# Which rows of a chunked scan TensorE transposes, and which go by VectorE transposes and DRAM

## The chip, the cores and the metric

The kernel runs on one core of one Trainium2 chip. The metric is device time of one launch in microseconds (us), the median over several executions. The work of a core is spread over TensorE (PE; its weight loads are listed apart as PEld), VectorE (DVE), ScalarE (ACT), GpSimd (POOL) and SyncE (SP). Each engine takes its own instructions strictly in the order in which they stand in the program and waits on semaphores for the others. Nearly all transfers of this kernel are issued from SP's queue.

## The reference

One step of a hybrid decoder layer in float32: RMSNorm, one wide projection, two branches (a Mamba-2 scan and a short gated convolution), a sigmoid-gated sum, an output projection and a last RMSNorm. There are 336 tokens: 16 learned ones and 256 of a prompt in one sequence, and 8 sequences of 8. The change touches the scan:

```python
xbc_c, conv_new = causal_dwconv(xbc, conv_prev, ssd_conv_w)
xbc = jax.nn.silu(xbc_c + ssd_conv_b)
xs, bm, cm = jnp.split(xbc, [D_INNER, D_INNER + SSD_GROUPS * SSD_STATE], axis=-1)
...
cb = jnp.einsum('bcign,bcjgn->bcijg', cc, bc)
wts = cb[..., None] * decay * dtc[:, :, None]
y_diag = jnp.einsum('bcijgr,bcjgrp->bcigrp', wts, xc)
chunk_states = jnp.einsum('bcjgr,bcjgrp,bcjgn->bcgrpn', to_end, xc, bc)
```

The projection leaves channels on the partitions and tokens along the row, and the convolution works that way. The products over tokens j need the same values with tokens on the partitions: xc (4 tiles of 128 channels in each of the 8 groups) and bc (one tile of 128 states). So five tiles of 128 channels x 336 tokens have to be turned in each group, in chunks of 128, 128 and 80 tokens.

## The kernel before, in words

All weights are split into two reduced-precision parts. A weight tile of 128 columns is read in two halves, which this text calls blocks and marks a and b. For one block, `wblk` loads 512 KB to `wraw` (line 92, SP), ACT rounds it to `whi` (line 94), DVE subtracts to `wlo` (line 96), and TensorE runs 16 matmuls with `whi` (lines 111 and 112) and then 8 with `wlo` (line 115). `wraw`, `whi` and `wlo` have three buffers each, so a block can be prepared while TensorE works on the blocks before it.

The scan runs in 8 stages, one for each group g. `weave` strings a stage's projections together: the gate z of group g (blocks z0a to z3b, the evacuation by ACT is lines 502 and 503), the output product of group g-1 (8 blocks), in two stages some branch gates, and then the projections of group g+1 with their convolution (`conv_tile`, blocks BTa to x3b). Between these units it places the steps of the generator `ssd(g)`, which yields after each step. `behind` ties the ACT, DVE and TensorE instructions of a step behind the latest block that was traced; within these ties a scheduler lays down each engine's final order when the program is built.

`conv_tile` projects, has ACT copy the result to a padded tile and apply the first tap with its bias (lines 462, 463, 469; tile `cacc`, two buffers), DVE add three taps (line 471), ACT take a tanh (line 474) and DVE write the result (lines 475, 476) to `BT`, `CT` or a quarter of `xs`.

In `ssd`, the steps `rows(0)`, `rows(1)`, `rows(2)` turn one chunk each: four transposes of `xs` by TensorE (line 534), one of `BT` (line 536), one product of B and C (line 537); DVE multiplies the turned x by dt to `xdt` (line 539), ACT and DVE split the turned B (lines 546, 547), DVE masks the product (line 551). `decay` and `weights` make the decay matrices, `state` and the 64 products of line 650 use them all. Near the stage's end stand the grouped norm (`ms_r`, lines 700 to 705; `yh`, `yl`, lines 726 to 728) and the states of the 8 short sequences, whose tiles `h` are loaded at line 607 (`h0T`, 4 transfers of 512 KB), added to at line 716 and stored at line 719 (`ssms`, 4 transfers of 512 KB). These transfers stand in SP's queue among the weight loads.

Of the kernel before, what the change touches and what calls it, by code (L numbers as in the profile page):

```python
# [7 lines left out]
F32 = mybir.dt.float32  # L8
F32R = mybir.dt.float32r
AF = mybir.ActivationFunctionType  # L10
# [3 lines left out]
P = 128  # L14
T = 336
# [7 lines left out]
HP = 64  # L23
# [4 lines left out]
DUM = 14  # L28
WARM = 10
NSTEP = 23  # L30

C_ID, C_U, C_M1, C_UQ, C_M1Q, C_ONE = 0, 128, 272, 400, 480, 560
C_SEG = 688
# [5 lines left out]
def fb(ap):  # L39
    return ap.bitcast(F32)  # L40


def bc(ap, shape):
    return ap.to_broadcast(shape)
# [3 lines left out]
def tile_hybrid_step(ctx, tc, xT, w0, w1, w2, wdt, wso, wsc, wo, cmask, vec, hvec, convst, sconvst, xe_, fwe, h0T,  # L48
                     yA, yB, yE, convo, ssmp, ssms, sconvo):
    nc = tc.nc  # L50
    mult, add, sub = ALU.mult, ALU.add, ALU.subtract
# [3 lines left out]
    ps = ctx.enter_context(tc.tile_pool(name="ps", bufs=2, space=PSUM))  # L55
    dr = ctx.enter_context(tc.tile_pool(name="dr", bufs=1, space=bass.MemoryType.DRAM))

    ac_d = [dr.tile([NH, n], F32, name=f"ac_d{c}") for c, n in enumerate((P - META, PX, 80))]
    mb_d = dr.tile([KT, P, TV], F32, name="mb_d")
    sg_d = dr.tile([KT, P, TV], F32, name="sg_d")  # L60
    xq_d = [dr.tile([80, 4, 512], F32, name=f"xq_d{i}") for i in range(2)]
    bq_d = [dr.tile([80, 4, P], F32, name=f"bq_d{i}") for i in range(2)]

# [11 lines left out]
    ident = CM[:, C_ID:C_ID + P]  # L75
# [12 lines left out]
    latest = {}  # L88

    def wblk(src, n=1024):  # L90
        raw = wp.tile([P, 1024], F32, name="wraw")
        nc.sync.dma_start(raw[:, :n], src)
        hi = wp.tile([P, 1024], F32R, name="whi")
        latest["act"] = nc.scalar.activation(hi[:, :n], raw[:, :n], AF.Copy).ins  # L94
        lo = wp.tile([P, 1024], F32R, name="wlo")
        latest["dve"] = nc.vector.tensor_tensor(lo[:, :n], raw[:, :n], fb(hi[:, :n]), sub).ins  # L96
        return hi, lo

    def behind(tail):
        for ins in reversed(nc.cur_bb.bb.instructions):  # L100
            if ins is tail:
                break
            for a in latest.values():
                if ins.engine == a.engine:
                    tc.add_manual_dep(ins, a.name, mybir.DependencyInfo(mybir.DependencyClass.NoSync,
                                                                         mybir.DependencyReason.DATA), reason="step")

    def mm(out, hi, lo, xh, xl, base, nk, k0, first, last):
        for k in range(nk):
# [14 lines left out]
    def proj(src, t0):  # L124
        return unit(src, lambda k: hhi[:, k, t0:T], lambda k: hlo[:, k, t0:T], T - t0)
# [35 lines left out]
    act = keep.tile([P, 3, NH], F32, name="act")  # L161
    dtt = keep.tile([P, 3, NH], F32, name="dtt")
# [7 lines left out]
    with tc.tile_pool(name="pa", bufs=2) as pa:  # L170
# [4 lines left out]
        raw = []  # L175
# [28 lines left out]
        for k in range(KT):  # L204
# [5 lines left out]
            if k % 2 == 0 or k == 1:  # L210
                o = slice(384 * k, 384 * k + 384) if k < 2 else slice(0, 768)
# [233 lines left out]
    def hv(ap, g):  # L445
        return ap[:, 8 * g:8 * g + 8].unsqueeze(2)

    with tc.tile_pool(name="pb", bufs=2) as pb:
# [5 lines left out]
        nc.gpsimd.memset(CZ, 0.0)  # L454
        czs = CZ.rearrange("p (s i w) -> p s i w", s=2, w=40)

        def conv_tile(src, j, t0, out, cs):
            pp = proj(src, t0)
            pad = pads[npad[0] % 2]
            npad[0] += 1  # L460
            smp = pad[:, 275:363].rearrange("p (b t) -> p b t", t=11)
            nc.scalar.activation(pad[:, 3 + t0:275], pp[:, :272 - t0], AF.Copy)  # L462
            nc.scalar.activation(smp[:, :, 3:11], pp[:, 272 - t0:].rearrange("p (b t) -> p b t", t=8), AF.Copy)
            nc.gpsimd.tensor_copy(smp[:, :, 0:3], cs[:, 1:9, :])  # L464
            nc.gpsimd.tensor_copy(cs[:, 0, :], pad[:, 272:275])  # L465
            nc.gpsimd.tensor_copy(cs[:, 1:9, :], smp[:, :, 8:11])
            i0 = META if t0 else 0
            acc = pb.tile([P, 360], F32, name="cacc")
            nc.scalar.activation(acc[:, i0:], pad[:, i0:360], AF.Identity, bias=col(V_CB, j), scale=col(V_CW, 4 * j))
            for k in range(1, 4):  # L470
                nc.vector.scalar_tensor_tensor(acc[:, i0:], pad[:, i0 + k:360 + k], col(V_CW, 4 * j + k),  # L471
                                               acc[:, i0:], mult, add)
            th = pb.tile([P, 360], F32, name="cth", bufs=1)
            nc.scalar.activation(th[:, i0:], acc[:, i0:], AF.Tanh)
            nc.vector.scalar_tensor_tensor(out[:, i0:272], th[:, i0:272], 1.0, acc[:, i0:272], add, mult)
            nc.vector.scalar_tensor_tensor(
                out[:, 272:].rearrange("p (b t) -> p b t", t=8),
                th[:, 272:360].rearrange("p (b t) -> p b t", t=11)[:, :, 3:11], 1.0,
                acc[:, 272:360].rearrange("p (b t) -> p b t", t=11)[:, :, 3:11], add, mult)

        def conv_units(g, st):
            cs = pb.tile([P, 6, 9, 3], F32, name="cs")
            nc.sync.dma_start(cs, convst[:, g])
            BT = st["BT"] = pb.tile([P, T], F32, name="BT")
            conv_tile(w1[64 + g], 32 + g, 0, BT, cs[:, 4])
            yield
            CT = st["CT"] = pb.tile([P, T], F32, name="CT")
            conv_tile(w1[72 + g], 40 + g, 12, CT, cs[:, 5])
            yield
            xs = st["xs"] = pb.tile([P, 4, T], F32, name="xs", tag=f"xs{g % 2}", bufs=1)  # L490
            for t in range(4):
                conv_tile(w1[32 + 4 * g + t], 4 * g + t, 0, xs[:, t, :], cs[:, t])
                yield
            nc.sync.dma_start(convo[:, g], cs)

# [12 lines left out]
        def big(tag, bufs, dt=F32):  # L508
            return pb.tile([P, 512], dt, name=tag, bufs=bufs)

        def split(ap, w=HP):
            return ap.rearrange("p (h e) -> p h e", e=w)

        def ssd(g, st):
# [3 lines left out]
            xw = free[:, :1024].rearrange("p (i n) -> p i n", n=512)  # L518
            h0, h0t = [], []
            ys = pb.tile([P, 4, T], F32, name="ys", bufs=1)  # L520
            W, xdt, xe, bt, cbm, hst = ([None] * 3 for _ in range(6))
            W[0], W[1] = (pb.tile([P, 8, PX], F32, name="W")[:, :, :n] for n in (P - META, PX))
            W[2] = pb.tile([P, 8, 80], F32, name="W2", bufs=1)
            E = pb.tile([P, 8, PX], F32, name="E", bufs=1)
# [2 lines left out]
                nc.sync.dma_start(w[:r], ac_d[c][8 * g:8 * g + 8, :].partition_broadcast(r))  # L527
            NT, TGT = (P - META, PX, 80), (META, P, 2 * P)

            def rows(c):  # L530
                (t0, n), m = CH[c], NT[c]
                pp = ps.tile([P, 512], F32, name="ms")
                for t in range(4):
                    nc.tensor.transpose(pp[:n, t * P:t * P + P], xs[:, t, t0:t0 + n], ident)  # L534
                pq = ps.tile([P, 512], F32, name="ms")
                nc.tensor.transpose(pq[:n, 0:P], BT[:, t0:t0 + n], ident)
                nc.tensor.matmul(pq[:n, P:P + m], BT[:, t0:t0 + n], CT[:, TGT[c]:TGT[c] + m], start=True, stop=True)
                xdt[c] = big("xdt", 3)
                nc.vector.tensor_tensor(split(xdt[c][:n]), split(pp[:n]), bc(hv(dtt[:n, c, :], g), [n, 8, HP]), mult)
                if c == 2:  # L540
                    bt[c] = pb.tile([P, P], F32, name="bt", bufs=1)
                    nc.scalar.activation(bt[c][:n], pq[:n, 0:P], AF.Copy)
                else:
                    bt[c] = (free[:, 1024:1280].rearrange("p (i n) -> p i n", n=P) if c else
                             pb.tile([P, 2, P], F32R, name="bh0", bufs=1))
                    nc.scalar.activation(bt[c][:, 0, :], pq[:, 0:P], AF.Copy)
                    nc.vector.tensor_tensor(bt[c][:, 1, :], pq[:, 0:P], fb(bt[c][:, 0, :]), sub)
                cbm[c] = pb.tile([P, PX], F32, name="cbm")
                u0 = META if c == 0 else 0
                for a, b, o in ((0, m, 0),) if c < 2 else ((META, 80, 0), (0, META, 64)):  # L550
                    nc.vector.tensor_tensor(cbm[c][:n, o:o + b - a], pq[:n, P + a:P + b],
                                            U[:, u0 + a:u0 + b] if c < 2 else UQ[:, a:b], mult)

            def decay(c):
                n, m, w = CH[c][1], NT[c], W[c]
                for h in range(8):
                    a = act[:n, c, 8 * g + h:8 * g + h + 1]
                    if c:
                        nc.scalar.activation(w[:n, h, :], w[:n, h, :], AF.Relu, scale=-1.0, bias=a)  # L559
                    else:  # L560
                        nc.vector.tensor_scalar(w[:n, h, :], w[:n, h, :], a, 0.0, sub, ALU.min)
                nc.scalar.activation(w[:n], w[:n], AF.Exp, scale=-1.0 if c else 1.0)
# [33 lines left out]
                    nc.gpsimd.tensor_tensor(split(h0[b]), split(h0[b]), bc(hv(decS[:, b, :], g), [P, 8, HP]), mult)  # L596

            yield
            rows(0)
            yield  # L600
            decay(0)
            yield
            nc.scalar.activation(E, W[1], AF.Exp)
            rows(1)
            for u in range(4):
                h = pb.tile([P, 2, 512], F32, name="h0", bufs=4)
# [429 lines left out]
```

## Time and profile before

| what | before |
|---|---|
| median of 3 runs | 1823.18 us (1822.88 to 1823.36) |
| profiled execution, its own time | 1824.75 us |
| its span, first to last instruction | 1823.0 us |
| TensorE busy | 1814.9 us of the span |
| VectorE busy | 1147.7 us |
| ScalarE busy | 828.8 us |
| granted TensorE clock | 1.0 |
| SP's DMA queue, share of 16 engines | 55.9% |

A row of the timeline reads: start in us from the span's start, length, engine, line and operation, what is written and read, how many equal ones follow each other, and in brackets how long the engine had been idle and what ended that. A row of a group gives the busy time in all and the mean of one in ns, then the idle time before it. "SPq" rows are DMA issues: their length is the issue, not the transfer. Matmuls overlap, so what one costs TensorE is read from the distance of two starts and not from its length.

### The profile page before, as it was taken

What the parts mean: (1) busy time and instruction counts of PE and PEld (TensorE: products, weight loads), DVE (VectorE), ACT (ScalarE), POOL (GpSimd) and SP (SyncE); (2) the same over time, 40 slices, a digit from 0 to 9 for tenths busy, and PEclk for the clock granted to TensorE, in tenths of its full rate; (3) what the DMA queues carried; (4) which work ended last, traced back from release to release, by engine and by line L of the source; (5) the groups of instructions that cost most, each with busy time, mean ns of one, the idle gap of its engine ahead of it and who ended that gap; (6) DMA issues with size and microseconds to landing.
All of it is one profiled execution on the core that took longest, in us unless ns stands there. A gap on an engine that the chain in (4) does not pass through costs nothing.

```text
span 1823.0 us, 32410 instructions
## 1 busy us (share of the span) xinstructions
PE 1814.9 (100%) x13006; PEld 1798.0 (99%) x13006; DVE 1147.7 (63%) x1696; ACT 828.8 (45%) x1269; POOL 389.4 (21%) x398
## 2 busy tenths in 40 slices
PE   9999999999999999999999999999999999999998
PEld 9999999999999999999999999999999999999998
DVE  7745544444543335668587787877778777776544
ACT  6433333333333334645656354564546545343543
POOL 0000000000000001253162433524334252400012
PEclk9999999999999999999999999999999999999999
DMA  7444444444444446457566574665656657476553
GB/s 254 146 151 150 150 149 149 145 152 151 156 152 159 160 162 227 149 178 240 163 201 223 177 246 150 208 215 178 238 157 211 206 169 249 153 243 213 184 175 129
DMA packets 117286, 331.33 MB, mean 182 GB/s; under 512 B 20944, under 2 KB 37904, under 8 KB 117136
## 3 DMA queue, kind: packets, MB, share of 16 engines
q1 hardware_dynamic: 116272, 327.89, 55.9%
q8 instruction: 102, 1.67, 0.4%
q10 hardware_dynamic: 864, 1.38, 0.2%
q14 instruction: 48, 0.39, 0.1%
HBM read 296.34 MB, written 32.88 MB: 181 GB/s over the span
## 4 chain that ended last, share of the span: by engine, by line
PE 96%; DMA 2%; ACT 1%; DVE 1%; issue 0%; POOLq 0%; POOL 0%; SPq 0%; ACTq 0%; DVEq 0%
PE pj L111 30%; PE pj L112 30%; PE pj L115 29%; PE yb L650 2%; DMA wraw<-w 1%; PE ms L636 1%; PE pj L219 1%; PE yb L585 1%; PE pj L862 1%; ACT whi L94 0%; PE ms L534 0%; ACT W L559 0%; PE ms L219 0%; DMA ssms<-h 0%; PE yb L713 0%
## 5 line engine op out<-in xcount | busy, mean ns | idle before, releaser
L111 PE MATMUL pj<-hx,whi 128*128 128x320 f32 (+3 forms) x2880 | 864.4, 312 | 0.0
L112 PE MATMUL pj<-hx,whi 128*128 128x320 f32 (+3 forms) x2880 | 860.6, 311 | 0.0
L96 DVE TENSOR_TENSOR wlo<-wraw,whi 128x1024 fp32r<-128x1024 f32 x470 | 596.8, 1270 | 413.9 <-ACT whi L94 206.8
L94 ACT ACTIVATE whi<-wraw 128x1024 fp32r<-128x1024 f32 x470 | 496.7, 1057 | 768.0 <-PE pj L112 628.1
L111 PEld LDWEIGHTS pj<-hx,whi 128*128 128x128 f32 x2880 | 540.7, 188 | 4.6 <-ACT pad L462 1.7
L112 PEld LDWEIGHTS pj<-hx,whi 128*128 128x128 f32 x2880 | 541.5, 188 | 0.1
L115 PE MATMUL pj<-hx,wlo 128*128 128x320 f32 (+3 forms) x2880 | 485.4, 310 | 0.0
L115 PEld LDWEIGHTS pj<-hx,wlo 128*128 128x128 f32 x2880 | 440.6, 188 | 0.0
L111 PE MATMUL pj<-yh,whi 128*128 128x320 f32 x512 | 153.5, 311 | 1.2 <-ACT zs L503 0.9
L112 PE MATMUL pj<-yl,whi 128*128 128x320 f32 x512 | 152.3, 309 | 0.0
L596 POOL TENSOR_TENSOR h<-h,decS 128x512 f32<-128x512 f32 x64 | 76.4, 1227 | 147.5 <-PE ms L636 147.5
L111 PEld LDWEIGHTS pj<-yh,whi 128*128 128x128 f32 x512 | 96.2, 188 | 3.1 <-ACT zs L503 1.4
L112 PEld LDWEIGHTS pj<-yl,whi 128*128 128x128 f32 x512 | 96.3, 188 | 0.6
L115 PE MATMUL pj<-yh,wlo 128*128 128x320 f32 x512 | 95.8, 309 | 0.0
L242 POOL COPY SCS<-up 128x2 f32<-128x2 f32 x16 | 18.2, 1139 | 359.2 <-DVE up L236 329.0
L744 DVE TENSOR_TENSOR yan<-yan,pj 128x320 f32<-128x320 f32 x112 | 54.2, 485 | 62.9 <-PE pj L115 61.3
L471 DVE SCALAR_TENSOR_TENSOR cacc<-pad,V,cacc 128x360 f32<-128x360 f32 (+1 forms) x144 | 89.5, 621 | 2.0
L464 POOL COPY pad<-cs 128x24 f32<-128x24 f32 x48 | 56.2, 1172 | 126.6 <-DVE cacc L471 115.5
L115 PEld LDWEIGHTS pj<-yh,wlo 128*128 128x128 f32 x512 | 80.4, 188 | 0.0
L111 PE MATMUL pj<-vhi,whi 128*128 128x320 f32 x256 | 75.5, 308 | 0.0
L112 PE MATMUL pj<-vlo,whi 128*128 128x320 f32 x256 | 75.5, 308 | 0.0
L465 POOL COPY cs<-pad 128x3 f32<-128x3 f32 x48 | 45.0, 938 | 82.5 <-ACT pad L462 82.0
(286 smaller groups left out, 1721.7 us busy)
## 6 DMA issues: line engine op xcount, KB each, us to landing
wraw<-w SPq DMA_DIRECT2D x346, 512.0 KB, 3.9
wraw<-wso SPq DMA_DIRECT2D x64, 512.0 KB, 3.5
wraw<-wsc SPq DMA_DIRECT2D x32, 512.0 KB, 3.8
h<-h0T SPq DMA_DIRECT2D x32, 512.0 KB, 4.9
ssms<-h SPq DMA_DIRECT2D x32, 512.0 KB, 4.2
wraw<-wo SPq DMA_DIRECT2D x32, 512.0 KB, 3.9
xq_d<-xe SPq DMA_DIRECT2D x16, 320.0 KB, 3.4
W<-ac_d SPq DMA_DIRECT2D x8, 576.0 KB, 6.4
```

Source lines behind the costliest of these rows:

```text
L94: latest["act"] = nc.scalar.activation(hi[:, :n], raw[:, :n], AF.Copy).ins
L96: latest["dve"] = nc.vector.tensor_tensor(lo[:, :n], raw[:, :n], fb(hi[:, :n]), sub).ins
L111: nc.tensor.matmul(out, w, xh(k0 + k), start=first and k == 0, stop=False)
L112: nc.tensor.matmul(out, w, xl(k0 + k), start=False, stop=False)
L115: latest["pe"] = nc.tensor.matmul(out, w, xh(k0 + k), start=False, stop=last and k == nk - 1).ins
L219: nc.tensor.matmul(pu[i][:, :T - t0], w[:, o:o + P], x[:, k, t0:], start=k == 0 and j == 0, stop=k == 15 and j == 2)
L464: nc.gpsimd.tensor_copy(smp[:, :, 0:3], cs[:, 1:9, :])
L465: nc.gpsimd.tensor_copy(cs[:, 0, :], pad[:, 272:275])
L471: nc.vector.scalar_tensor_tensor(acc[:, i0:], pad[:, i0 + k:360 + k], col(V_CW, 4 * j + k), acc[:, i0:], mult, add)
L596: nc.gpsimd.tensor_tensor(split(h0[b]), split(h0[b]), bc(hv(decS[:, b, :], g), [P, 8, HP]), mult)
L650: nc.tensor.matmul(yb[q * HP:(q + 1) * HP, t, t0:t0 + n], x[:, h * HP:(h + 1) * HP], w[:, h, :], start=i == 0, stop=i == 3)
L744: nc.vector.tensor_tensor(ya[:, m, :TV], ya[:, m, :TV], pp[:, :TV], add)
```

## The change

B and the first two of the four x tiles are turned another way. After their convolution, DVE transposes the tile in 32x32 squares (two instructions, one of 320 columns and one of 32) into the tile `cacc`, and four DMAs write the squares to a scratch tensor in DRAM, `xr_d` (352 rows of 384 floats, in pieces of 32 floats), so that its rows are tokens. `pend` holds each tile's writes back until two more tiles have been projected, and `after` ties them behind the latest weight load of that moment. A new function `load` reads a chunk's rows back to `xdt` and to the B tile in three steps of the stage; `decay(0)` moves one step forward. `rows` keeps two TensorE transposes and the product of B and C, and multiplies x by dt in two halves. `behind` ties the same three engines as before.

```diff
     def wblk(src, n=1024):
         raw = wp.tile([P, 1024], F32, name="wraw")
-        nc.sync.dma_start(raw[:, :n], src)
+        latest["sp"] = nc.sync.dma_start(raw[:, :n], src).ins
...
-        def conv_tile(src, j, t0, out, cs):
+        pend = []
+
+        def conv_tile(src, j, t0, out, cs, rows=None):
             pp = proj(src, t0)
+            for p in pend:
+                p[0] -= 1
+            while pend and not pend[0][0]:
+                _, to, frm = pend.pop(0)
+                for a in range(0, P, 32):
+                    after(nc.sync.dma_start(to[:, :, a:a + 32], frm[a:a + 32]).ins, latest["sp"])
...
+            if rows is not None:
+                nc.vector.transpose(acc[:, :320], out[:, :320])
+                nc.vector.transpose(acc[:, 320:XR], out[:, T - 32:])
+                pend.append([2, rows.rearrange("(b q) c -> q b c", q=32),
+                             acc[:, :XR].rearrange("p (b f) -> p b f", f=32)])
...
-            conv_tile(w1[64 + g], 32 + g, 0, BT, cs[:, 4])
+            conv_tile(w1[64 + g], 32 + g, 0, BT, cs[:, 4], xr_d[g % 2][:, 256:])
...
-                conv_tile(w1[32 + 4 * g + t], 4 * g + t, 0, xs[:, t, :], cs[:, t])
+                conv_tile(w1[32 + 4 * g + t], 4 * g + t, 0, xs[:, t, :], cs[:, t],
+                          xr_d[g % 2][:, P * t:P * t + P] if t < 2 else None)
...
+            def load(c):
+                xdt[c] = big("xdt", 3)
+                b = bt[c] if c == 2 else fb(bt[c][:, 1, :])
+                for o, r, n in ((0, P * c, P),) if c < 2 else ((0, 256, 64), (64, 336, 16)):
+                    for d, q in ((xdt[c][:, :256], slice(0, 256)), (b, slice(256, 384))):
+                        after(nc.sync.dma_start(d[o:o + n], xr_d[g % 2][r:r + n, q]).ins, latest["sp"])
+
             def rows(c):
                 (t0, n), m = CH[c], NT[c]
                 pp = ps.tile([P, 512], F32, name="ms")
-                for t in range(4):
-                    nc.tensor.transpose(pp[:n, t * P:t * P + P], xs[:, t, t0:t0 + n], ident)
-                pq = ps.tile([P, 512], F32, name="ms")
-                nc.tensor.transpose(pq[:n, 0:P], BT[:, t0:t0 + n], ident)
-                nc.tensor.matmul(pq[:n, P:P + m], BT[:, t0:t0 + n], CT[:, TGT[c]:TGT[c] + m], start=True, stop=True)
-                xdt[c] = big("xdt", 3)
-                nc.vector.tensor_tensor(split(xdt[c][:n]), split(pp[:n]), bc(hv(dtt[:n, c, :], g), [n, 8, HP]), mult)
...
+                for t in range(2):
+                    nc.tensor.transpose(pp[:n, t * P:t * P + P], xs[:, t + 2, t0:t0 + n], ident)
+                nc.tensor.matmul(pp[:n, 256:256 + m], BT[:, t0:t0 + n], CT[:, TGT[c]:TGT[c] + m], start=True, stop=True)
+                for x, y, h in ((split(xdt[c][:n, :256]),) * 2 + (0,), (split(xdt[c][:n, 256:]), split(pp[:n, :256]), 4)):
+                    nc.vector.tensor_tensor(x, y, bc(dtt[:n, c, 8 * g + h:8 * g + h + 4].unsqueeze(2), [n, 4, HP]), mult)
+                if c < 2:
+                    b = fb(bt[c][:, 1, :])
+                    nc.scalar.activation(bt[c][:, 0, :], b, AF.Copy)
+                    nc.vector.tensor_tensor(bt[c][:, 1, :], b, fb(bt[c][:, 0, :]), sub)
...
             yield
-            rows(0)
+            load(0)
+            decay(0)
             yield
-            decay(0)
+            load(1)
+            rows(0)
             yield
             nc.scalar.activation(E, W[1], AF.Exp)
+            load(2)
             rows(1)
```

The scheduler makes more of it than the diff shows: other instructions change places too. Three places matter below. The rows are those of stages 1 and 2; stages 0 to 7 repeat the pattern (the first two places between two stages, the third in stages 1 to 7).

VectorE, from the projection of x2 to that of x3 (`wlo_9588`, `wlo_9618`, `wlo_9683` are the blocks x2a, x2b and x3a; `cacc_9653` is x2's convolution; the change's line numbers are 2 to 26 higher). Of the change, the end of the stretch:

```order
L494 STREAM_TRANSPOSE cacc_9561<-xs_9396 128x320
L495 STREAM_TRANSPOSE cacc_9561<-xs_9396 128x32
L752 SCALAR_TENSOR_TENSOR ys_8539<-ys_8539,V_77,ms_r_9485 128x320
L754 TENSOR_TENSOR yl_9665<-ys_8539,yh_9664 128x320
L752 SCALAR_TENSOR_TENSOR ys_8539<-ys_8539,V_77,ms_r_9485 128x320
L754 TENSOR_TENSOR yl_9665<-ys_8539,yh_9664 128x320
L752 SCALAR_TENSOR_TENSOR ys_8539<-ys_8539,V_77,ms_r_9485 128x320
L484 SCALAR_TENSOR_TENSOR cacc_9653<-pad0_6711,V_77,cacc_9653 128x360
L754 TENSOR_TENSOR yl_9665<-ys_8539,yh_9664 128x320
L484 SCALAR_TENSOR_TENSOR cacc_9653<-pad0_6711,V_77,cacc_9653 128x360
L754 TENSOR_TENSOR yl_9665<-ys_8539,yh_9664 128x320
L484 SCALAR_TENSOR_TENSOR cacc_9653<-pad0_6711,V_77,cacc_9653 128x360
```

Right behind the last of these stands `wlo_9683`. Before, x3a's `wlo` (there `wlo_9635`) stood ahead of two of the four `yl` steps and of all three steps of x2's convolution, there were no transposes, and x2a's `wlo` stood ahead of the norm's first step (`ms_x`, line 701); in the change it stands behind that step and seven more. On TensorE the 16 `whi` matmuls of z0a now stand between x3a's `whi` and `wlo` matmuls, where before x3a's 24 stood together.

ScalarE, among the gate blocks of a stage (`whi_9969`, `whi_10029`, `whi_10059` are z2b, z3a, z3b; `pj_9936` is z2's projection, `pj_9845` that of z1). Of the change:

```order
L521 ACTIVATE cth_9907<-pj_9845 128x320
L522 ACTIVATE zs_9906<-pj_9845 128x320
L96 ACTIVATE whi_9969<-wraw_9967 128x1024
L628 ACTIVATE E_9839<-W_9837 128x1152
L569 ACTIVATE xw_9834<-xw_9834 128x128
L521 ACTIVATE cth_9998<-pj_9936 128x320
L522 ACTIVATE zs_9997<-pj_9936 128x320
L96 ACTIVATE whi_10029<-wraw_10027 128x1024
```

Of before (`whi_9914`, `whi_9973` are z2b and z3a, `pj_9791` is z1's projection):

```order
L94 ACTIVATE whi_9914<-wraw_9912 128x1024
L603 ACTIVATE E_9787<-W_9785 128x1152
L94 ACTIVATE whi_9973<-wraw_9971 128x1024
L502 ACTIVATE cth_9853<-pj_9791 128x320
L503 ACTIVATE zs_9852<-pj_9791 128x320
```

z3a's `whi` stood ahead of the evacuation of z1, and now stands behind that of z2, the projection that TensorE ends just before z3.

SP, from z0b on (`wraw_9798` is z0b, 9846 and 9876 are z1, 9937 and 9967 z2, 10027 z3a). Of the change:

```order
L94 DMA wraw_9876<-w1 128x1024
L546 DMA W_9837<-ac_d1_67 128x1152
L513 DMA convo<-cs_9199 128x162
L557 DMA xdt_9911<-xr_d0_71 128x256
L745 DMA ssms<-h0_8726 128x1024
L745 DMA ssms<-h0_8728 128x1024
L557 DMA bh0_9843<-xr_d0_71 128x128
L557 DMA xdt_9923<-xr_d0_71 128x256
L557 DMA xw_9834<-xr_d0_71 128x128
L94 DMA wraw_9937<-w1 128x1024
```

Behind them come z2b's load, four small loads of chunk 2, all four loads of `h0T` and then z3a's load. Before, z2a's load stood ahead of `convo`, z2b's and the second pair of `ssms` behind it, and two loads of `h0T` had been issued before z0b's load, the other two between z3a's and z3b's. The writes of `xr_d` stand behind x1b's load (B) and z0a's load (x0 and x1, around the first pair of `ssms`).

More of the change, by code (lines that the diff above doesn't have):

```diff
@@ L30 @@
 NSTEP = 23
+XR = 352
 C_ID, C_U, C_M1, C_UQ, C_M1Q, C_ONE = 0, 128, 272, 400, 480, 560
@@ L60, in tile_hybrid_step @@
     sg_d = dr.tile([KT, P, TV], F32, name="sg_d")
+    xr_d = [dr.tile([XR, 384], F32, name=f"xr_d{i}") for i in range(2)]
     xq_d = [dr.tile([80, 4, 512], F32, name=f"xq_d{i}") for i in range(2)]
@@ L97, in wblk, with after @@
         return hi, lo
+    def after(ins, a):
+        tc.add_manual_dep(ins, a.name, mybir.DependencyInfo(mybir.DependencyClass.NoSync,
+                                                            mybir.DependencyReason.DATA), reason="step")
     def behind(tail):
@@ L102, in behind @@
                 break
[L103 to L106, printed above, removed]
+            for k in ("act", "dve", "pe"):
+                if k in latest and ins.engine == latest[k].engine:
+                    after(ins, latest[k])
     def mm(out, hi, lo, xh, xl, base, nk, k0, first, last):
@@ L520, in ssd @@
             ys = pb.tile([P, 4, T], F32, name="ys", bufs=1)
-            W, xdt, xe, bt, cbm, hst = ([None] * 3 for _ in range(6))
+            W, xdt, xe, cbm, hst = ([None] * 3 for _ in range(5))
             W[0], W[1] = (pb.tile([P, 8, PX], F32, name="W")[:, :, :n] for n in (P - META, PX))
@@ L528, in ssd @@
             NT, TGT = (P - META, PX, 80), (META, P, 2 * P)
+            bt = [pb.tile([P, 2, P], F32R, name="bh0", bufs=1), free[:, 1024:1280].rearrange("p (i n) -> p i n", n=P),
+                  pb.tile([P, P], F32, name="bt", bufs=1)]
+            def load(c):
[4 more added lines that the diff above has]
+                        after(nc.sync.dma_start(d[o:o + n], xr_d[g % 2][r:r + n, q]).ins, latest["sp"])
             def rows(c):
@@ L532, in rows @@
                 pp = ps.tile([P, 512], F32, name="ms")
-                for t in range(4):
-                    nc.tensor.transpose(pp[:n, t * P:t * P + P], xs[:, t, t0:t0 + n], ident)
-                pq = ps.tile([P, 512], F32, name="ms")
-                nc.tensor.transpose(pq[:n, 0:P], BT[:, t0:t0 + n], ident)
-                nc.tensor.matmul(pq[:n, P:P + m], BT[:, t0:t0 + n], CT[:, TGT[c]:TGT[c] + m], start=True, stop=True)
-                xdt[c] = big("xdt", 3)
-                nc.vector.tensor_tensor(split(xdt[c][:n]), split(pp[:n]), bc(hv(dtt[:n, c, :], g), [n, 8, HP]), mult)
[L540 to L547, printed above, removed]
+                for t in range(2):
[7 more added lines that the diff above has]
+                    nc.vector.tensor_tensor(bt[c][:, 1, :], b, fb(bt[c][:, 0, :]), sub)
                 cbm[c] = pb.tile([P, PX], F32, name="cbm")
@@ L550, in rows @@
                 for a, b, o in ((0, m, 0),) if c < 2 else ((META, 80, 0), (0, META, 64)):
-                    nc.vector.tensor_tensor(cbm[c][:n, o:o + b - a], pq[:n, P + a:P + b],
+                    nc.vector.tensor_tensor(cbm[c][:n, o:o + b - a], pp[:n, 256 + a:256 + b],
                                             U[:, u0 + a:u0 + b] if c < 2 else UQ[:, a:b], mult)
@@ L598, in ssd @@
             yield
+            load(0)
+            decay(0)
+            yield
+            load(1)
             rows(0)
             yield
-            decay(0)
-            yield
             nc.scalar.activation(E, W[1], AF.Exp)
+            load(2)
             rows(1)
```

## The prediction

> **What bounds the kernel now.** I read the page first: its busy times and the chain of work that ended last.
>
> ```profile
> PE 1814.9 (100%) x13006; PEld 1798.0 (99%) x13006; DVE 1147.7 (63%) x1696; ACT 828.8 (45%) x1269; POOL 389.4 (21%) x398
> ...
> PE 96%; DMA 2%; ACT 1%; DVE 1%; issue 0%; POOLq 0%; POOL 0%; SPq 0%; ACTq 0%; DVEq 0%
> ```
>
> TensorE never rests. The list of its waits shows the same; these four are all:
>
> ```profile
> PE ms L188 <- DVE warm L173: 1.2, 1, 1.2
> PE pj L111 <- ACT zs L503: 0.9, 1, 0.9
> PE pj L827 <- POOL rs_r L823: 0.3, 1, 0.3
> PE pj L111 <- DVE yan L744: 0.3, 1, 0.3
> ```
>
> So time taken from TensorE is gained in full, and each wait that the change puts ahead of it is lost in full. The question is how much the other queues hold in reserve where the change presses on them, and the timeline of one stage tells that. I take the stretch from the end of stage 1 to the middle of stage 2.
>
> **What is gained.** Per chunk three of five transposes go: 9 a stage, 72 in all. TensorE's own rows at the first chunk, between z1b and z2a (the second stands between z2b and z3a):
>
> ```profile
> 974.90 0.60 PE L534 MATMUL ms<-CR,xs 128*128 128x128 f32 x4
> 975.34 0.27 PE L536 MATMUL ms<-CR,BT 128*128 128x128 f32 x1
> 975.45 0.37 PE L537 MATMUL ms<-CT,BT 128*128 128x112 f32 x2
> 975.59 0.39 PE L111 MATMUL pj<-hx,whi 128*128 128x320 f32 x1
> ```
>
> Five transposes move the next start from 974.90 to 975.45: 0.55 us, 0.11 each. 72 x 0.11 = 7.9 us less. The group row of x's transposes gives another figure, the mean length of one:
>
> ```profile
> L534 PE MATMUL ms<-CR,xs 128*128 128x128 f32 (+1 forms) x96 | 14.4, 272 | 0.0
> ```
>
> 272 ns is a length, and the lengths overlap; I take the distance. [...]
>
> **What is added, place one: x3a's `wlo`.** DVE's rows near a stage's end (the `wlo` rows are x2b, x3a, x3b):
>
> ```profile
> 939.42 0.49 DVE L701 TENSOR_SCALAR ms_x<-ms 128x320 f32<-128x320 f32 x1 [1.11 <-ACT ms_r L700]
> ...
> 943.07 1.22 DVE L96 TENSOR_TENSOR wlo<-wraw,whi 128x1024 fp32r<-128x1024 f32 x1
> 944.21 0.48 DVE L704 TENSOR_TENSOR ms_a<-ms_a,ms_r 128x320 f32<-128x320 f32 x1
> ...
> 950.80 0.49 DVE L728 TENSOR_TENSOR yl<-ys,yh 128x320 fp32r<-128x320 f32 x1
> 951.20 0.43 DVE L475 SCALAR_TENSOR_TENSOR xs<-cth,cacc 128x272 f32<-128x272 f32 x1
> ...
> 953.02 1.21 DVE L96 TENSOR_TENSOR wlo<-wraw,whi 128x1024 fp32r<-128x1024 f32 x1
> ...
> 954.96 0.58 DVE L471 SCALAR_TENSOR_TENSOR cacc<-pad,V,cacc 128x360 f32<-128x360 f32 x1
> 955.47 1.21 DVE L96 TENSOR_TENSOR wlo<-wraw,whi 128x1024 fp32r<-128x1024 f32 x1
> ```
>
> From the norm's first step at 939.42, which waits for ACT and cannot come sooner, DVE works without a gap until x3a's `wlo` ends at 954.23. TensorE needs it here:
>
> ```profile
> 952.80 0.32 PE L111 MATMUL pj<-hx,whi 128*128 128x336 f32 x1
> ...
> 955.28 0.62 PE L115 MATMUL pj<-hx,wlo 128*128 128x336 f32 x3
> ```
>
> The reserve is 1.05 us. By the order of the change there now stand in this gapless stretch, beyond what stood there: x2a's `wlo` (1.14, as x2b's from 943.07 to 944.21), two `yl` steps (950.80 to 951.20: 0.40 each, 0.80), three steps of x2's convolution (954.96 to 955.47: 0.51 each, 1.53) and two pairs of 32x32 transposes. The trace has one such transpose:
>
> ```profile
> L643 DVE STREAM_TRANSPOSE xe<-xe 128x256 f32<-128x256 f32 x8 | 3.6, 446 | 0.3
> ```
>
> 446 ns for 256 columns makes 0.56 for 320; with the short one and overlap between neighbours I take 0.57 a pair (between 0.45 and 0.75), 1.14 for two. In all 4.6 us: x3a's `wlo` starts at 957.6 and ends at 958.8. TensorE meanwhile does z0a's 16 `whi` matmuls first; x3a's 16 took 952.80 to 955.28, and at 320 columns instead of 336 they take 2.36, so the need moves to 957.64. A wait of **1.2 us** remains, 0.9 to 1.5 by the price of a pair. It can be more: x2's first convolution step now also waits until x0's four writes have left the `cacc` buffer. The last of them is issued near 950 (x0 is turned at 947.2 by the sum above, and a store of the state stands between the four). For its landing the nearest rows are a 64-row write, a write of 160 pieces of 512 bytes, and a load of 1024 pieces:
>
> ```profile
> ac_d<-acx SPq DMA_DIRECT2D x1, 4.0 KB, 1.7
> bq_d<-bhh SPq DMA_DIRECT2D x16, 80.0 KB, 3.8
> W<-ac_d SPq DMA_DIRECT2D x8, 448.0 KB, 5.7
> ```
>
> 1.7 to 5.7; with 352 pieces and 44 KB nearest to the middle one, 3.8, so they land at 953.8, before DVE reaches the step (955.3). At 5.7 ACT's first step (0.69) would end at 956.4 and add 1.1. [...]
>
> **Place two: z3a's `whi`.** ACT now evacuates z2 (two instructions) ahead of z3a's `whi`. z2 ends on TensorE just before the second chunk's transposes, and z3a starts behind them. How fast ACT answers and how it proceeds, from TensorE's end of x1 and from z1's evacuation:
>
> ```profile
> 944.54 0.40 PE L585 MATMUL ms<-xdt,b 128*128 128x512 f32 x1
> ...
> 944.80 0.40 ACT L462 ACTIVATE pad<-pj 128x272 f32<-128x272 f32 x1 [0.23 <-PE pj L115]
> ...
> 974.45 1.06 ACT L94 ACTIVATE whi<-wraw 128x1024 fp32r<-128x1024 f32 x1 [0.49 <-DMA wraw<-w]
> 975.42 0.42 ACT L502 ACTIVATE cth<-pj 128x320 f32<-128x320 f32 x1
> 975.73 0.43 ACT L503 ACTIVATE zs<-pj 128x320 f32<-128x320 f32 x1
> 976.05 0.28 ACT L546 ACTIVATE bh<-ms 128x128 fp32r<-128x128 f32 x1
> ```
>
> ACT starts 0.26 after TensorE's next instruction; 0.31 and 0.32 for the two steps, 1.06 for `whi`: it is ready 1.95 after z2's end. TensorE fills 0.36 of that (two transposes, 0.22, and the product, 975.45 to 975.59). **1.6 us** of wait remain in each of stages 1 to 7, whatever the loads do. Before, this `whi` (the 974.45 row) was ready 8 us ahead. DVE has a like pattern, z2a's and z3a's `wlo` behind the chunk's dt products, but 16 `whi` matmuls of 0.15 stand in front of that need; I count nothing.
>
> **Place three: the loads of z2a and z3a.** SP's rows before:
>
> ```profile
> 954.30 6.82 SPq L92 DMA_DIRECT2D wraw<-w  x4
> ...
> 965.72 1.97 SPq L719 DMA_DIRECT2D ssms<-h  x2
> 968.99 0.34 SPq L92 DMA_DIRECT2D wraw<-w  x1
> 971.90 1.30 SPq L607 DMA_DIRECT2D h<-h0T  x2
> 973.30 0.37 SPq L92 DMA_DIRECT2D wraw<-w  x1
> ```
>
> z2a's load was the last of the four from 954.30; z3a's is the 968.99 row and lands at 974.45 (the ACT row), 5.4 later, behind two stores. Now z2a's load stands behind the second pair of stores, which wait for DVE's additions to `h`. Those come after z0b's `wlo`, whose load waits for x3a's `wlo` (958.8), takes 4.1 (954.30 to this row),
>
> ```profile
> 958.44 1.06 ACT L94 ACTIVATE whi<-wraw 128x1024 fp32r<-128x1024 f32 x1 [3.92 <-DMA wraw<-w]
> 964.48 1.21 DVE L716 TENSOR_TENSOR h<-h,yb 128x1024 f32<-128x1024 f32 x1
> 966.12 1.21 DVE L716 TENSOR_TENSOR h<-h,yb 128x1024 f32<-128x1024 f32 x1
> 980.61 1.06 ACT L94 ACTIVATE whi<-wraw 128x1024 fp32r<-128x1024 f32 x1 [4.28 <-DMA wraw<-w]
> ```
>
> then 1.06 for `whi` and 1.2 for `wlo`: 965.2. Two convolution steps and two additions (964.48 to 966.12 is one of each) make 968.5 to 969. Three small loads follow, some 0.5 each, so z2a's load goes out at 970.6 and, with 5.4, lands at 976.0; `whi` is ready at 977.1. TensorE wants it at 975.59 + 1.2 (place one) - 0.33 (three transposes) = 976.4, and has to load a weight first: **1.0 us**, between 0 and 2.5, since the sum is long.
>
> z3a's load stands behind all four loads of `h0T`, and the last of these needs the semaphore of z2b's load, so it goes out when that has landed, near 978. Before, three 512 KB transfers landed between the ACT rows 974.45 and 980.61: 2.05 each. Five from 978 at 1.5 to 2.05 land at 985.5 to 988.3. With place two, `whi` could start 0.89 after z2's end, and z2a's start moved by 1.9 puts that at 985.5. **1.0 us** more, between 0 and 2.8; nearer the lower end, as some of the four run while SP waits.
>
> The other edits cost nothing: DVE's extra transposes of B fall where `wlo` has 8 us in hand, ACT loses one copy, the small loads carry little.
>
> **Sum.** -7.9 + 7 x (1.2 + 1.6 + 1.0 + 1.0) = -7.9 + 33.6 = +25.7 us. On the profiled execution's 1824.75 that is 1850.5; this one lies 1.57 above the median of the runs, 1823.18, so the forecast is **1849 us**. The bounds together: -7.9 + 7 x (0.9 + 1.6) = +9.6 gives 1833, and -7.9 + 7 x (2.6 + 1.6 + 2.5 + 2.8) = +58.6 gives 1882.
>
> **The rivals.**
> *Only z3a's `whi` waits.* Place one is covered (transposes cheap, DVE's gapless stretch starts sooner) and the loads are in time. -7.9 + 7 x 1.6 = +3.3: 1826. For it: long sums of small steps err, and the reserves elsewhere were 5 us or more. Against it: x3a's reserve was the smallest of the stage already. 15%.
> *The loads decide.* Small writes are slow, SP is held, and every later load with it: the upper bounds, 1882 and about. For it: SP's queue now mixes stores, lane waits and weights; against it: the DMA engines were 56% busy. 12%.
> *Faster: a transpose costs TensorE its length.* 72 x 0.272 = 19.6 us are freed instead of 7.9. It decides where a stage's waits stay under 2.8 us: with z3a's wait alone, 1823.2 - 19.6 + 11.2 = 1815. Against it: the distances above. [...] 6%.
>
> **How the numbers follow.** The forecast's own case (1833 to 1868) has 67%. The range 1826 to 1872 leaves out the faster rival, most of the load rival and the tail. A difference under 0.2% (3.6 us) can't be told from none here. Faster: the third rival, 6%. Within 0.2%: two fifths of the first rival, whose 1826.5 lies at that edge, 6%. Slower: 88%.
>
> **What would show it.** In the profile after: 48 rows on the transposes of x and none of B. The list of TensorE's waits names `whi` (ACT) and `wlo` (DVE) with seven or more cases each, the first with about 1.6 us or more a case at z3a, the second with about 1.2 at x3a. DMA as releaser of ACT's `whi` grows from z2a on. If TensorE's waits stay at the 2.7 us of before, my reading of the orders is wrong; if they sum to 11, the first rival holds.

## The result, and the profile after

The change made the kernel slower: 1849.53 us (1848.06 to 1850.6) against 1823.27, a ratio of 1.0144 with a 95% interval of 1.0131 to 1.0156. The forecast was 1849. Measured times are medians; one run of experiment 8, of 8628.74 us where its others took 1862 to 1869, is left out of them. The profiled execution took 1849.81 us, its span is 1848.0, 25.0 more than before. TensorE now waits; its list of waits in the kernel after:

```profile
PE pj L116 <- ACT whi L96: 15.4, 12, 1.9
PE pj L120 <- DVE wlo L98: 6.8, 8, 0.9
PE ms L193 <- DVE warm L178: 1.2, 1, 1.2
PE pj L116 <- ACT zs L522: 1.2, 1, 1.2
PE pj L116 <- DVE yan L770: 0.5, 2, 0.3
PE pj L853 <- POOL rs_r L849: 0.3, 1, 0.3
```

(The columns: who waits for whom; us in total, cases, the longest.) The two lists that the prediction named are there, `whi` with 12 cases and `wlo` with 8. In the timeline they stand at the three places and hardly anywhere else: x3a's `wlo` in stages 0 to 6, 0.93 or 0.94 each (one more `wlo` wait of 0.24 stands elsewhere); z2a's `whi` in five of the stages 1 to 7, 0.55 to 1.22; z3a's `whi` in all seven, 1.33 to 1.93.

**Place one**, between stages 1 and 2, DVE's rows and the wait that ends them on TensorE:

```profile
942.04 0.49 DVE L727 TENSOR_SCALAR ms_x<-ms 128x320 f32<-128x320 f32 x1 [4.03 <-ACT ms_r L726]
...
949.26 0.51 DVE L494 STREAM_TRANSPOSE cacc<-xs 128x320 f32<-128x320 f32 x1
...
949.78 0.56 DVE L484 SCALAR_TENSOR_TENSOR cacc<-pad,V,cacc 128x360 f32<-128x360 f32 x1
...
960.08 1.21 DVE L98 TENSOR_TENSOR wlo<-wraw,whi 128x1024 fp32r<-128x1024 f32 x1
...
961.35 1.51 PE L120 MATMUL pj<-hx,wlo 128*128 128x336 f32 x8 [0.93 <-DVE wlo L98]
```

From the norm's first step (942.04) DVE works without a gap to x3a's `wlo` (960.08). That is 18.0 us; the prediction's stretch was 939.42 to 957.6, 18.2. Before, it was 13.6 (939.42 to 953.02). A pair of 32x32 transposes takes 0.52 (949.26 to 949.78), 0.57 was assumed.

**Place two**, z3a of stage 2, ACT's rows, the TensorE rows around them, and the load's (SP):

```profile
980.88 1.48 SPq L94 DMA_DIRECT2D wraw<-w  x2
...
987.26 0.38 PE L563 MATMUL ms<-CR,xs 128*128 128x128 f32 x2
987.48 0.41 PE L564 MATMUL ms<-CT,BT 128*128 128x144 f32 x2
...
987.46 0.44 ACT L521 ACTIVATE cth<-pj 128x320 f32<-128x320 f32 x1 [4.52 <-PE pj L120]
987.80 0.43 ACT L522 ACTIVATE zs<-pj 128x320 f32<-128x320 f32 x1
988.12 2.18 ACT L96 ACTIVATE whi<-wraw 128x1024 fp32r<-128x1024 f32 x2
...
989.23 0.41 PE L116 MATMUL pj<-hx,whi 128*128 128x320 f32 x1 [1.33 <-ACT whi L96]
```

ACT had been idle for 4.52 us when z2 ended, and then did z2's two steps before `whi`. Without the wait z3a would have started 0.36 after 987.26, by the prediction's rows at 987.62; it started at 989.23, 1.61 later. The list says 1.33: the last matmul's length covers 0.28 more. So the rest of the text counts each listed wait as itself and some 0.28, an estimate from this case.

**Place three**, z2a of stage 2:

```profile
969.74 1.97 SPq L745 DMA_DIRECT2D ssms<-h  x2
971.75 0.72 SPq L557 DMA_DIRECT2D bh<-xr_d  x1
...
973.71 0.85 SPq L94 DMA_DIRECT2D wraw<-w  x2
...
979.03 1.06 ACT L96 ACTIVATE whi<-wraw 128x1024 fp32r<-128x1024 f32 x1 [1.53 <-DMA wraw<-w]
...
980.14 0.41 PE L116 MATMUL pj<-hx,whi 128*128 128x320 f32 x1 [0.81 <-ACT whi L96]
```

The second pair of stores waits for DVE until 969.74, z2a's load goes out behind it at 973.71, and ACT, idle for 1.53, takes up the tile when it has landed.

### The profile page after: what moved, and what is told of

Its sections match the earlier page's. It is cut to its first block, busy times and chain, and to the rows that moved or that the text cites. A ratio compares the mean times of both kernels' runs of the same rounds, so it can differ in the third digit from the quotient of the medians.

```text
span 1848.0 us, 32573 instructions
## 1 busy us (share of the span) xinstructions
PE 1817.0 (98%) x12934; PEld 1794.3 (97%) x12934; DVE 1180.0 (64%) x1768; ACT 830.1 (45%) x1261; POOL 393.6 (21%) x398
## 5 line engine op out<-in xcount | busy, mean ns | idle before, releaser
L477 POOL COPY pad<-cs 128x24 f32<-128x24 f32 x48 | 85.0, 1773 | 140.2 <-DVE cacc L484 131.8
L247 POOL COPY SCS<-up 128x2 f32<-128x2 f32 x16 | 18.2, 1139 | 359.2 <-DVE up L241 329.0
L591 POOL TENSOR_TENSOR xe<-xdt,tet 128x512 f32<-128x512 f32 (+1 forms) x24 | 30.8, 1282 | 123.0 <-DVE xdt L566 80.9
```

The source lines that it names most:

```text
L591: nc.gpsimd.tensor_tensor(split(xe[c][:n]), split(xdt[c][:n]), bc(hv(tet[:n, c, :], g), [n, 8, HP]), mult)
```

## The experiments

The theory is that of the prediction: the order of three queues costs the time, not the added work. The rival is the work itself: the DVE transposes and the small transfers. A third question is the gain, 0.11 or 0.27 us a transpose.

**1. The gain alone.** In the kernel before:

```diff
-                for t in range(4):
-                    nc.tensor.transpose(pp[:n, t * P:t * P + P], xs[:, t, t0:t0 + n], ident)
+                for t in range(2):
+                    nc.tensor.transpose(pp[:n, t * P:t * P + P], xs[:, t + 2, t0:t0 + n], ident)
...
-                nc.tensor.transpose(pq[:n, 0:P], BT[:, t0:t0 + n], ident)
```

> The kernel before with the 72 transposes left out and nothing in their place: the x products of the first two tiles and the splits of B read the transposed columns of the third tile instead, so the time is read and not the values; the dt product is done in two halves as in the change. The order of ACT, DVE and SP around the stage's end is that of before. Theory (a transpose costs TensorE 0.11 us, the distance of starts): 1823.3 - 7.9 = 1815.4, and no new waits of TensorE. Rival (it costs its length, 0.272): 1803.7. Second rival (TensorE's time falls but a new wait takes it): 1819 or more, with waits above 2.7 us in the list.

Measured: 1816.2 us (1815.5 to 1818.21), ratio 0.9963 (0.9948 to 0.9978); its waits:

```profile
PE ms L188 <- DVE warm L173: 1.2, 1, 1.2
PE pj L828 <- POOL rs_r L824: 0.3, 1, 0.3
```

7.0 us less than the 1823.16 of before beside it, 0.10 a transpose, with no new wait. The two profiles differ by 9.1 us (spans 1813.9 and 1823.0), of which 1.7 are the two waits of before for `zs` and `yan`, which are gone here; the 7.4 left are 0.10 a transpose as well. The figure of 0.272 would have given 1803.7 and is out.

**2. The writes on another queue.** One line of the change:

```diff
-                    after(nc.sync.dma_start(to[:, :, a:a + 32], frm[a:a + 32]).ins, latest["sp"])
+                    nc.scalar.dma_start(to[:, :, a:a + 32], frm[a:a + 32])
```

> The change with one edit: the writes of the squares go out on ACT's queue instead of SP's. All DVE transposes, all bytes and all loads of rows stay. By its order, x2a's wlo and x2's convolution stand where they stood before the change, z3a's whi stands ahead of z2's evacuation again, two h0T loads go out before z0b's load; but z1b's load now stands behind the second pair of stores. Theory (the added time is the order of the queues, at three places): the wait at x3a falls from 0.93 to under 0.4, that at z3a from 1.3 to 1.9 to under 0.7, a wait at z1b or z2a of up to 2 may remain; 1815 to 1835. Rival (the added work itself: 96 DVE transposes, the small transfers): 1843 to 1850, since all of it is still there.

Measured: 1822.6 us (1821.17 to 1823.37), ratio to before 0.9994 (0.9985 to 1.0003), so 27 us less than the change. The waits at x3a and z3a are gone:

```profile
PE pj L116 <- ACT whi L96: 3.2, 6, 0.7
PE ms L193 <- DVE warm L178: 1.2, 1, 1.2
PE pj L853 <- POOL rs_r L849: 0.3, 1, 0.3
```

All six are at z1b. Every transpose on DVE (48 instructions more than before; the 96 of the expectation are the writes), every byte and every load is still there, and the time is that of before. This decides against the work as the cause. The scheduler reacts to the queue on which the writes stand, and lays down x3a, z3a and `h0T` nearly as before. DVE's reserve at x3a, though, is down to 0.08 us:

```profile
1064.38 1.22 DVE L98 TENSOR_TENSOR wlo<-wraw,whi 128x1024 fp32r<-128x1024 f32 x1
...
1065.67 1.48 PE L120 MATMUL pj<-hx,wlo 128*128 128x336 f32 x8
```

**3. x alone.** B is turned by TensorE as before:

```diff
-            conv_tile(w1[64 + g], 32 + g, 0, BT, cs[:, 4], xr_d[g % 2][:, 256:])
+            conv_tile(w1[64 + g], 32 + g, 0, BT, cs[:, 4])
...
+                pq = ps.tile([P, 512], F32, name="ms")
+                nc.tensor.transpose(pq[:n, 0:P], BT[:, t0:t0 + n], ident)
```

> The change without its part on B: TensorE transposes B as before (24 come back), x's first two tiles keep the new way. By its order DVE is back to the order of before at x3a, with x0's and x1's transposes still in the stretch; z3a's whi stands behind the evacuations of z1 and z2 and behind a split of B; all four h0T loads stand ahead of z3a's load. Theory: no wait over 0.4 at x3a; at z3a 1.3 to 2.0 in each of seven stages; -48 x 0.11 = -5.3, so 1823.3 - 5.3 + 7 x (1.6 to 3) = 1829 to 1839. Rival (the added work): two thirds of 33.6 us stay, 1840, with about 0.6 to 0.9 at x3a.

Measured: 1837.87 us (1837.05 to 1838.46), ratio 1.0079 (1.0064 to 1.0095).

```profile
PE pj L116 <- ACT whi L96: 14.6, 14, 1.4
```

No wait at x3a, though both pairs of transposes are in the stretch; 1.39 at z3a in each of seven stages, as DVE's and ACT's orders said. x3a's `wlo` ends 0.07 us ahead of its need (956.36 for 956.43). The other seven cases are at z1b, whose load stands behind the second pair of stores here; I had not counted those.

**4. The loads of `h0T` first.**

```diff
+            for u in range(4):
+                h = pb.tile([P, 2, 512], F32, name="h0", bufs=4)
+                nc.sync.dma_start(h, h0T[g, :, 2 * u:2 * u + 2, :])
+                ...
             yield
             load(0)
```

(with the same lines removed from the fourth step)

> The change with one edit: the four loads of h0T stand at the head of the stage's steps instead of in the fourth. By its order z3a's whi stands ahead of z2's evacuation again, z3a's load only behind four small loads; z2a's load stands behind two h0T loads, z1a's behind two others; DVE's order at x3a is that of the change. Theory: x3a still waits 0.93 in each of seven cases; z3a's 1.3 to 1.9 fall under 0.7; z2a's 0.5 to 1.2 stay or grow to 2.5; in all 1836 to 1849. Rival (z3a waits for its load alone, whatever ACT's order): z3a's wait goes too, but only as far as its load lands sooner, and the evacuation's place makes no difference.

Measured: 1882.18 us (1877.03 to 1886.94), ratio 1.0313 (1.0295 to 1.0332). A miss by over 30 us. SP's rows and the waits show why:

```profile
1087.22 0.35 SPq L94 DMA_DIRECT2D wraw<-w  x1
1087.67 0.85 SPq L623 DMA_DIRECT2D h<-h0T  x2
1092.90 0.33 SPq L546 DMA_DIRECT2D W<-ac_d  x1
1093.73 0.34 SPq L513 DMA_DIRECT2D convo<-cs  x1
1094.19 0.36 SPq L94 DMA_DIRECT2D wraw<-w  x1
```

```profile
PE pj L116 <- ACT whi L96: 41.5, 14, 5.1
PE pj L120 <- DVE wlo L98: 6.6, 7, 0.9
```

z1a's load (1094.19), which in the change went out 1.6 us behind z0b's in the same stage (1077.27 and 1078.90), now goes out 7.0 behind it: two loads of `h0T`, a load of W and `convo` stand between, and SP issued the five in that order, z1a's 0.46 behind `convo` (1093.73). The two loads of `h0T` go out at once. It is the load of W that waits until 1092.90, by the trace for TensorE's products of the short sequences (30.5 us in seven cases), and `convo` until 1093.73 for GpSimd. So z1a waits 2.9 to 5.1. The other seven cases are z2a's, 1.4 to 4.0, behind the other two loads of `h0T`, which wait for the stores `ssms` (26.4 us in 14 cases), and four small loads. z3a does not wait any more, and x3a's seven cases are unchanged at 0.93 to 0.94, as expected. Whether z3a owes that to ACT's order or to a TensorE that comes later, this run can't tell.

**5. ACT's order alone.** The kernel before, and one tie that keeps z3a's `whi` behind z2's evacuation:

```diff
+                k = len(blocks)
                 pz = proj(w1[4 * g + t], META)
+                if g and t == 3:
+                    after(blocks[k][0], last)
...
-                nc.scalar.activation(z[:, :TV], pz, AF.Copy)
+                last = nc.scalar.activation(z[:, :TV], pz, AF.Copy).ins
```

> The kernel before with one tie more: z3a's whi stands behind the evacuation of z2 on ACT, as in the change. Nothing else of the change is in it; DVE's, SP's and TensorE's orders are those of before, all transposes stay on TensorE. Theory (this order alone costs): TensorE fills the time with five transposes instead of two, so of the 1.33 us of wait that the change showed where its load was in time 1.0 remains, plus some 0.28 until TensorE is at its spacing again, in seven stages: 1823.2 + 7 x 1.28 = 1832, and no other wait. Rival (the buffers hold enough, the wait in the change came from the late load): 1823.

Measured: 1838.47 us (1836.74 to 1840.47), ratio 1.0084 (1.007 to 1.0097).

```profile
PE pj L116 <- ACT whi L94: 7.0, 7, 1.0
PE pj L116 <- ACT zs L511: 2.8, 6, 0.7
```

Seven waits of 1.00 us, as worked out, in a kernel whose loads, transposes and DVE order are those of before. This settles place two: the position of one instruction on ACT, 1.28 a stage here. The six others were not foreseen: ACT, pushed back, evacuates z3 late as well, and the output products behind it wait. Both kinds together are 9.8 + 13 x 0.28 = 13.4; less 1.7 for the two waits of before, and with the 0.5 of the one that is left, 12.2, and the profile's span grew by 12.0 (1823.0 to 1835.0). Two of the four runs took some 3.5 us more than the profiled one, which this profile does not show.

**6. The second pair of stores later,** with the writes on ACT's queue as in 2:

```diff
                 for b in range(2):
-                    nc.sync.dma_start(ssms[g, :, 4 * u + 2 * b:4 * u + 2 * b + 2, :], h0t[2 * u + b])
+                    late.append((ssms[g, :, 4 * u + 2 * b:4 * u + 2 * b + 2, :], h0t[2 * u + b]))
+                if u == 0 or g == NG - 1:
+                    store()
...
             yield
+            store()
             load(0)
```

(`store` issues what `late` holds, behind the latest weight load)

> As the second experiment (writes on ACT's queue), and the second pair of stores of ssms is issued in the second step of the next stage, which puts it behind z1b's load instead of ahead of it. Theory: the six waits of 0.3 to 0.7 at z1b go, some 5 us with their restarts; z2a's load, now behind the stores and four small loads, may wait 0 to 0.5; so 1816 to 1820, against 1816.2 with the transposes simply left out. Rival (what the second experiment lost against that 1816.2 is the added DVE and DMA work): 1822 to 1823 again.

Measured: 1819.34 us (1817.51 to 1821.11), ratio 0.9978 (0.9969 to 0.9987): some 4 us below before and 30 below the change.

```profile
PE ms L193 <- DVE warm L178: 1.2, 1, 1.2
PE pj L116 <- ACT whi L96: 1.1, 1, 1.1
```

z1b's waits are gone. Some 3 us to the 1816.2 of the first experiment are left; 1.4 of them is the one wait, the rest I did not assign.

**7. B alone.**

```diff
-                          xr_d[g % 2][:, P * t:P * t + P] if t < 2 else None)
+                          None)
...
-                for t in range(2):
-                    nc.tensor.transpose(pp[:n, t * P:t * P + P], xs[:, t + 2, t0:t0 + n], ident)
+                for t in range(4):
+                    nc.tensor.transpose(pp[:n, t * P:t * P + P], xs[:, t, t0:t0 + n], ident)
```

> The change with its part on B alone: 24 transposes go, x is turned by TensorE as before. By its order x2a's wlo is late and z0a's whi matmuls stand between x3a's, as in the change, but without x0's and x1's transposes in the stretch; z3a's whi stands behind z2's evacuation; z2a's load behind the second pair of stores and two small loads, z3a's behind two small loads and two of h0T. Theory: no wait at x3a (0.93 less two pairs of transposes, 1.1); z2a 0 to 0.5; z3a 1.33 in each of seven stages; -24 x 0.11 = -2.6; 1823.2 - 2.6 + 7 x (1.6 to 2.1) = 1832 to 1836. Rival (the added work): a third of it, 1832, but spread as in the change, with 0.3 at x3a and 0.5 at z3a.

Measured: 1825.22 us (1823.01 to 1829.23), ratio 1.0014 (1.0005 to 1.0023). A miss at z3a, by my reading of the order: the two evacuation rows that I took for z2's are z1's. The timeline of ACT shows it:

```profile
978.39 0.41 ACT L521 ACTIVATE cth<-pj 128x320 f32<-128x320 f32 x1
978.71 0.42 ACT L522 ACTIVATE zs<-pj 128x320 f32<-128x320 f32 x1
980.02 1.06 ACT L96 ACTIVATE whi<-wraw 128x1024 fp32r<-128x1024 f32 x1 [0.89 <-DMA wraw<-w]
...
985.22 0.41 ACT L521 ACTIVATE cth<-pj 128x320 f32<-128x320 f32 x1
```

z3a's `whi` (980.02) stands ahead of z2's evacuation (985.22), and TensorE's list has two waits for `whi`, 0.8 us in all. So with the right order ACT's cost is gone, as the theory has it. No wait at x3a in the list, as expected, but this run has only a part of the change's order there: x2a's `wlo` is late and one `yl` step more stands ahead, while x2's convolution stands behind x3a's `wlo` again and three of z0a's matmuls, not 16, between x3a's. That part, without x's transposes, leaves 0.05 us; experiment 3, the transposes without the order, leaves 0.07. So either uses up the reserve of 1.05 and no more. That place one takes both is the sum's reading; the change's whole order without the transposes was not run.

**8. The stores later, with the writes left on SP.** As 6 without the edit of 2, and with `store()` in the fourth step of the next stage:

```diff
             load(2)
+            store()
             rows(1)
```

> The change (writes on SP) with the second pair of stores of ssms issued in the fourth step of the next stage, which puts it behind z2b's load: z2a's load no longer stands behind it, z3a's load stands behind it and behind all four loads of h0T. DVE's and ACT's orders at x3a and z3a are those of the change. Theory: x3a waits 0.93 as before; z2a's wait (0.5 to 1.2) goes; z3a's grows from 1.3 to 1.9 to between 1.9 and 3.5, since its load goes out later; 1843 to 1856. Rival (z2a waits for something else, ACT's evacuation or the small loads): z2a's wait stays.

Measured: 1867.99 us (1862.42 to 1868.77), ratio 1.0236 (1.0221 to 1.0252). A miss by 12 us.

```profile
978.53 0.83 SPq L537 DMA_DIRECT2D ssms<-h  x2
979.41 4.48 SPq L641 DMA_DIRECT2D h<-h0T  x4
984.00 1.08 SPq L94 DMA_DIRECT2D wraw<-w  x2
```

```profile
PE pj L116 <- ACT whi L96: 28.2, 7, 5.3
PE pj L120 <- DVE wlo L98: 6.5, 7, 0.9
```

z2a does not wait in any stage: its wait in the change came from the second pair of stores. z3a's load goes out behind six transfers of 512 KB, at 984.00, and TensorE waits 3.3 to 5.3 in all seven stages, more than the 1.9 to 3.5 expected; the half clock (0.99 in the mean of the profiled run) adds to the miss, by the estimate at the end. x3a is unchanged.

## Why the prediction was right, step by step

The terms against the trace of the kernel after, each wait with its 0.28:

| term | predicted | measured |
|---|---|---|
| 72 transposes | -7.9 | -7.0 (experiment 1) |
| x3a's `wlo` | 7 x 1.2 = 8.4 | 7 x 1.21 = 8.5 |
| z3a's `whi`, ACT's order | 7 x 1.6 = 11.2 | 1.61 where ACT decides alone; 7 x 1.61 = 11.3 |
| z3a's load on top | 7 x 1.0 = 7.0 | 1.6 in all, in four stages |
| z2a's load | 7 x 1.0 = 7.0 | 5 cases, 4.5 + 5 x 0.28 = 5.9 |
| half clock behind two waits | not foreseen | 3.1 |
| one wait for `zs`, two for `yan`, one more for `wlo` | not foreseen | 3.0, against 1.7 for `zs` and `yan` before |
| sum | 25.7 | 24.7 of the 25.0 by which the span grew |

- **What is gained** held: distance, not length.
- **Place one** held: 18.0 us for 18.2 in its stretch, 0.93 + 0.28 for 1.2 in its wait. The transfers of x0 did not hold up x2's convolution. The page's issue row of the writes:

```profile
xr_d<-cacc SPq DMA_DIRECT2D x96, 44.0 KB, 2.3
```

  2.3 us, where 3.8 was taken from three rows of 1.7 to 5.7.
- **Place two** held: 1.61 where 1.6 was worked out, and experiment 5 shows it alone.
- **Place three, z2a,** held in its chain. Experiment 8 shows that its cause is the second pair of stores. Seen from x3a's start, 2.62 later in this stage (955.42 for 952.80), the load goes out at 971.1 for the 970.6 forecast and `whi` is ready at 977.5 for 977.1. It waits in five stages, not seven.
- **Place three, z3a's load,** is the term that was mis-sized: 1.6 us in place of 7.0. I took 1.0 between 0 and 2.8; in stage 2 the load had landed when ACT came free (no idle time ahead of 988.12), so it lay at the lower end. ACT's part of this was right: it came free at 988.12, and 985.5 was forecast for a stage that started 2.62 sooner. The transfers were faster than taken: z2b's load landed at 980.42 and z3a's, the fifth behind it, at 987.94, 1.50 each, the lower bound of 1.5 to 2.05. Where the load came last, the list has 1.42 to 1.93 in place of 1.33. Experiment 8 shows how near the other side was: with two stores ahead of it the same load cost 3.3 to 5.3.
- The half clock was not in the prediction at all. Both of its stretches (a granted clock of 0.50 for 3.4 us each) stand behind z3a waits that the load had lengthened (1.93 and 1.80), so the late load cost 3.1 more, by a way that the prediction lacked. The time came within 0.5 us of the forecast because the half clock and the unforeseen waits, some 4.4, stand against the 5.4 that the load's term was too large; the gain, 0.9 too large, and z2a, 1.1 too large, cancel as well. The places were foreseen; that the sum agrees so closely is luck.
- **The rivals.** Only z3a's wait (1826) fell with x3a's seven cases. The loads decide (1882) did not happen, but experiment 4 reaches its time by moving one group of transfers, and experiment 8 comes to 1868. A transpose that costs its length fell with experiment 1.

## What to carry to other kernels

When the bound engine never rests, a change's price is read from the orders that the scheduler makes of it: here three positions, one on each of DVE, ACT and SP, cost some 27 us of waits, and moving the new writes to another queue gave all but some 5 of them back (six waits, 3.2 + 6 x 0.28) without removing any work. On a queue such as SP's, where in experiment 4 z1a's load went out 7.0 us behind z0b's, look for the transfer that waits (a store that waits for a result, a load that waits for a buffer) and count which weight loads stand behind it. A buffer with little reserve (1.05 us at x3a, where `wlo` of most other blocks of that stage was ready 5 to 9 us ahead of its need) is where small additions on a free engine first show.

## What the runs showed that I had not expected

Two waits of TensorE cost more than their length: the granted clock halved behind them. After z3a's wait of 1.93 us in stage 4 it is 0.50 for 3.4 us (1221.0 to 1224.4), and the matmuls stand 0.27 apart in place of 0.15. TensorE's rows, then two rows of the table by windows (from the right: GB/s, DMA share, granted clock):

```profile
1220.94 0.61 PE L116 MATMUL pj<-hx,whi 128*128 128x320 f32 x1 [1.93 <-ACT whi L96]
...
1222.15 0.47 PE L116 MATMUL pj<-hx,whi 128*128 128x320 f32 x1
1222.42 0.47 PE L117 MATMUL pj<-hx,whi 128*128 128x320 f32 x1
...
1226.11 0.31 PE L116 MATMUL pj<-hx,whi 128*128 128x320 f32 x1
...
1229.62 0.31 PE L116 MATMUL pj<-yh,whi 128*128 128x320 f32 x1
```

```profile
1222.00:1224.00 2.00, 2.00 (x9) 2.00 (x8) 1.95 (x3) 2.00 (x7) 1.23 (x1) 0.50 0.29 45
1226.00:1228.00 2.00, 2.00 (x15) 2.00 (x15) 1.56 (x2) 2.00 (x3) 0.00 (x0) 1.00 0.39 156
```

The block took 5.17 us (1220.94 to 1226.11), the next one 3.51 (to 1229.62), and z3a of stage 2, at full clock behind its wait, 3.63: so 1.5 are the half clock's, and the same again in stage 6, where the clock is 0.50 from 1453.1 to 1456.5, behind z3a's wait of 1.80.

The length of the wait alone does not tell which ones these are. Behind z3a's wait of 1.81 in stage 1 (its row starts at 874.58) the granted clock stayed at 1.00 and the matmuls at 0.15, and so it was behind all shorter waits of the kernel after but the 1.80. What sets the 1.80 apart from the 1.81 was not shown.

In experiments 4 and 8, with waits of up to 5.1 and 5.3 us, the mean granted clock of the profiled run was 0.986 and 0.99, against 0.998 in the kernel after and 1.0 before. Behind a wait of 2.94 in experiment 4 the matmuls stand 0.26 apart (1113.60 and 1113.86). Waits and gain alone explain 45 of the 62 us by which the span grew in the first, and 30 of 43 in the second; that the half clock accounts for the 17 and 13 left is my estimate from these differences.
